# GpSimd's subtractions for the low parts of weights and rows, made in pieces of 256 columns

## The chip, the core and the metric

The kernel runs on one core of a Trainium2 chip. Five engines work side by side from queues of their own: TensorE (PE, matrix products), VectorE (DVE), ScalarE (ACT), GpSimd (POOL) and SyncE (SP), which here only issues transfers. An engine takes its instructions in program order and waits at one until the others that it needs have signalled. The metric is the device time of one execution in microseconds (us), and three runs of a kernel are summed up by their median.

## What is computed

Two layers of a diffusion backbone act on 512 latent tokens of width 1024, with 256 context tokens. The first layer mixes tokens by windowed attention with sink logits, the second by chunked spatial gating, and a SwiGLU block follows each. Every half layer is scaled and shifted by vectors that come from the conditioning vector.

```python
for i in range(DEPTH):                      # DEPTH = 2
    mod_l = silu_c @ ada_w[i] + ada_b[i]    # shift, scale, gate: 6 x 1024
    h_l = modulate(rmsnorm(x, norm_g[i, 0]), sh_ml, sc_ml)
    if kind == 0:
        y_l, y_c = window_sink_mixer(h_l, h_c, a_w_qkv[j], a_w_o[j], ...)
    elif kind == 1:
        y_l, y_c = chunk_gmlp_mixer(h_l, h_c, b_w_in[j], ..., b_w_o[j], ctx_out)
    x = x + g_ml * rmsnorm(y_l, norm_g[i, 1])
    f_l = swiglu(modulate(rmsnorm(x, norm_g[i, 2]), sh_fl, sc_fl), ffn_w_in[i], ffn_w_out[i])
    x = x + g_fl * rmsnorm(f_l, norm_g[i, 3])
```

All of it is float32.

## The kernel before, in words

**A product in three.** TensorE takes a faster float32 form (F32R) that keeps fewer bits, so an operand is split into a high part, which is the operand rounded to that form, and a low part, which is the operand less its high part. A product is then high x high + low x high + high x low, three matmuls (`mm3`, L267 to L270). `high` (L215) is a copy on ACT. `low` (L218) is a subtraction, L219 in the profile, on DVE unless the caller names another engine.

**Who names GpSimd.** Three callers do, and they stand in two stages of the first layer.

- Stage 1 multiplies the latent rows and the context rows by the key and value weights (`kv`, L572), one eighth of the width after the other, while the conditioning vectors of the next eighths are made. Its weights come in units of 128 x 2048, each in two halves of 128 x 1024. After the high part of a half (`ws.high`), `ws.low` makes the low part on GpSimd in one instruction of 1024 columns (L693); there are five such. One `kv` uses 512 columns of such a half.
- Attention works on four blocks of 128 queries and four groups of heads. In between, the query weights and part of the output weights are made ready: GpSimd subtracts halves of 512 columns (L1033 and L1061), fourteen in all.
- `Ada.stack` (L397) splits the summed rows of a conditioning vector, 64 partitions of 1024 columns, three times (`acc_st`; two in attention, one after it).

**The order.** In these two stages the order of the work is written out by hand: `at(time, step, ...)` puts a step into a plan under a name, a table ORDER ranks the names, and `run_plan` emits the steps by rank (a step that the table lacks comes behind, by its time). That is the order on every engine's queue; the times have no other effect.

**What the prediction speaks of.** `norm_in` (L476) scales half the width of a block of 128 context rows, `xin`, on DVE, and `turn_in` (L499) transposes it on TensorE. `modulate0` and `modulated_low` make the high and low parts `HA` of the modulated latent rows; `ada0_done` (L540 and L541) makes their scale and shift from small columns. `Ada.add` (L370) adds up weighted rows of the conditioning weights, loaded as `ada_raw` by SyncE through `dma` (L213). `k_add` (L795) finishes the rotated keys `kr`, which `k_turn` (L808) transposes to `kT`. In attention `rotate` (L726) multiplies queries by the rotary table on GpSimd, `q_split` (L747) subtracts on DVE, `normalise` (L927) multiplies probabilities `p` by the inverse sum on GpSimd, and `turn` (L933) transposes them on TensorE.

Of the kernel before, what the change touches and what calls it, by code (L numbers as in the profile page):

```python
# [7 lines left out]
F32 = mybir.dt.float32  # L8
# [3 lines left out]
ALU = mybir.AluOpType  # L12
# [190 lines left out]
def backbone_kernel(ctx: ExitStack, tc: tile.TileContext, a, out):  # L203
    nc = tc.nc
# [11 lines left out]
        nc.scalar.copy(out=hi, in_=src)  # L216

    def low(lo, hi, src, eng=None):  # L218
        (eng or nc.vector).tensor_tensor(out=lo, in0=src, in1=hi.bitcast(F32), op=ALU.subtract)  # L219

    def split(hi, lo, src):
        high(hi, src)
        low(lo, hi, src)
# [56 lines left out]
    class Stream:  # L280
# [37 lines left out]
        def low(self, u, h, eng, c0=0, c1=D):  # L318
            hi, lo = self.halves[u, h]
            low(lo[:, c0:c1], hi[:, c0:c1], self.raws[u][:, h * D + c0:h * D + c1], eng)  # L320
# [32 lines left out]
    class Ada:  # L353
# [32 lines left out]
        def halve(self, c, eng, of=stage):  # L386
            self.stages[c] = st = of("acc_st")
            high(st[:, 0:512], self.acc[:, c:c + 512])
            low(st[:, 512:], st[:, 0:512], self.acc[:, c:c + 512], eng)
# [280 lines left out]
    for k in range(KC):  # L670
        b, n = start[k], start[k + 1]
        for t in range(NT):
            at(b + .64 * t, kv, k, t)
        for z in ([k - 1] if k else []) + ([k] if k == KC - 1 else []):
            c = b if z < k else b + 1.3
# [303 lines left out]
    c = LEAD  # L979
# [113 lines left out]
    x = hb.tile([P, NT, D], F32, name="x")  # L1093
# [800 lines left out]
    for t in range(NT):  # L1894
        c = VChain(t)
# [149 lines left out]
```

## Time and profile before

| what | value |
|---|---|
| three runs | 1111.84, 1112.92, 1114.41 us; median 1112.92 |
| the profiled execution | 1113.02 us, of which its span is 1111.3 |
| granted clock of TensorE, mean | 0.995 |
| busy: PE, DVE, ACT, POOL | 1088.7, 951.4, 613.0, 246.4 us |
| instructions of POOL | 239 |
| GpSimd's subtractions, L219 | 5 of 128x1024, 14 of 128x512, 3 of 64x1024; 39.3 us together |

The first page gives each engine's busy time. A view by stretch gives the same for a part of the span. A view of groups puts instructions of one line, engine and shape together: their busy time, the mean of one in ns, then the engine's idle time just before them and what ended it. A row of the timeline is a start in us, a duration in us, the engine, the line, the operation, its output and inputs, and in square brackets the idle time before it and what released it; a row of "x2" is two instructions back to back. The chain of waits follows the work that ended last back to what released it. Matmuls overlap, so a matmul of 0.39 us may follow another by 0.23.

### The profile page before, as it was taken

How to read it: one execution, taken by the hardware profiler on the slowest of the kernel's cores; microseconds unless marked ns; L12 is line 12 of the kernel's file. 1: busy time of each engine (PE TensorE's matmuls, PEld its weight loads, DVE VectorE, ACT ScalarE, POOL GpSimd, SP SyncE). 2: the span in 40 equal slices, each digit the busy share in tenths (PEclk: the TensorE clock that was granted, in tenths of full speed). 3: DMA queues.
4: the chain of work that ended last, by engine and by line, in shares of the span. 5: the costliest groups of instructions: out<-in, count | busy, mean ns of one | idle time of the engine just before them, and what ended most of it. 6: DMA issues, size and time to landing. Idle time of an engine off the chain costs nothing.

```text
span 1111.3 us, 17832 instructions
## 1 busy us (share of the span) xinstructions
PE 1088.7 (98%) x6972; PEld 956.4 (86%) x6972; DVE 951.4 (86%) x1417; ACT 613.0 (55%) x1059; POOL 246.4 (22%) x239
## 2 busy tenths in 40 slices
PE   7999999999999999999999999999999999999997
PEld 4688887768899999998888788888899999998876
DVE  5788989868999999997987877988988898879985
ACT  6346777756555555555665634327555545546652
POOL 1316485533700000000320501006500000002400
PEclk9999999999999999999999999999999999999999
DMA  9543432153145556459973286652133343369911
GB/s 367 225 165 106 159 108 81 69 174 114 63 166 190 183 179 208 142 171 314 240 138 114 76 313 214 219 200 96 64 126 135 133 149 120 130 216 321 171 33 75
DMA packets 49016, 179.68 MB, mean 162 GB/s; under 512 B 4890, under 2 KB 9242, under 8 KB 37796
## 3 DMA queue, kind: packets, MB, share of 16 engines
q1 hardware_dynamic: 41300, 163.60, 42.3%
q0 software_dynamic: 7632, 14.95, 7.9%
q8 instruction: 54, 0.88, 0.3%
q14 instruction: 30, 0.25, 0.1%
HBM read 171.71 MB, written 2.10 MB: 156 GB/s over the span
## 4 chain that ended last, share of the span: by engine, by line
PE 84%; DVE 7%; DMA 3%; issue 2%; ACT 2%; POOL 1%; SPq 0%; DVEq 0%; POOLq 0%; ACTq 0%
PE f L1444 33%; PE y L1622 12%; PE y L276 5%; PE v L276 4%; PE y L1649 3%; PE s_ps L900 3%; PE o_ps L953 3%; PE pT_ps L933 3%; DVE w_lo L219 1%; PE u L1856 1%; PE u L1858 1%; PE u L1857 1%; PE q_ps L268 1%; DMA acc<-acc 1%; PE q_ps L270 1%
## 5 line engine op out<-in xcount | busy, mean ns | idle before, releaser
L1444 PE MATMUL f<-H,w_hi 128*128 128x256 f32 x960 | 178.4, 284 | 0.2 <-DVE fc L1455 0.2
L1444 PEld LDWEIGHTS f<-H,w_hi 128*128 128x128 f32 x960 | 149.9, 192 | 1.1 <-DVE fc L1455 0.7
L1444 PE MATMUL f<-H,w_lo 128*128 128x256 f32 x480 | 135.8, 283 | 0.0
L1622 PE MATMUL y<-w_hi,s 128*128 128x512 f32 x448 | 120.1, 389 | 0.0
L1444 PE MATMUL f<-S,w_hi 128*128 128x256 f32 x640 | 118.6, 283 | 0.0
L216 ACT CAST w_hi<-T 128x1024 fp32r<-128x1024 f32 x80 | 83.7, 1047 | 54.1 <-PE f L1444 35.0
L216 ACT CAST w_hi<-w_raw 128x1024 fp32r<-128x1024 f32 x90 | 94.4, 1052 | 30.0 <-PE y L1622 8.9
L1451 ACT COPY fc<-f 128x256 f32<-128x256 f32 x120 | 44.8, 373 | 103.0 <-PE f L1444 100.1
L219 DVE TENSOR_TENSOR w_lo<-w_raw,w_hi 128x1024 fp32r<-128x1024 f32 (+1 forms) x81 | 95.3, 1182 | 6.0 <-ACT w_hi L216 6.0
L1444 PEld LDWEIGHTS f<-S,w_hi 128*128 128x128 f32 x640 | 100.0, 192 | 0.1
L1622 PEld LDWEIGHTS y<-w_hi,s 128*128 128x128 f32 x448 | 84.1, 188 | 17.5
L219 DVE TENSOR_TENSOR w_lo<-T,w_hi 128x1024 fp32r<-128x1024 f32 x80 | 97.4, 1217 | 0.0
L1444 PEld LDWEIGHTS f<-H,w_lo 128*128 128x128 f32 x480 | 92.1, 192 | 0.0
L392 POOL DMA_DIRECT2D acc<-acc x9 | 7.8, 861 | 377.4 <-DVE acc L378 371.7
L1444 PE MATMUL f<-S,w_lo 128*128 128x256 f32 x320 | 90.6, 283 | 0.5 <-DVE w_lo L219 0.5
L378 DVE SCALAR_TENSOR_TENSOR acc<-ada_k,sc,acc 128x1024 f32<-128x1024 f32 x56 | 71.6, 1279 | 10.4 <-DMA ada_k<-in_ada 8.4
L1610 POOL DMA_DIRECT2D t<-in_w x48 | 42.2, 929 | 125.9 <-DMA t<-in_w 58.3
L1622 PE MATMUL y<-w_lo,s 128*128 128x512 f32 x224 | 69.1, 390 | 0.6 <-DVE w_lo L219 0.6
L1444 PE MATMUL f<-H,x 128*128 128x256 f32 x480 | 64.2, 283 | 0.0
L927 POOL TENSOR_SCALAR p<-p,st 128x512 f32<-128x512 f32 (+1 forms) x64 | 53.1, 845 | 47.0 <-DVE st L923 16.2
L276 PE MATMUL y<-w_hi,st 128*128 128x512 f32 x224 | 62.3, 391 | 0.0
L1444 PEld LDWEIGHTS f<-S,w_lo 128*128 128x128 f32 x320 | 61.4, 192 | 0.7 <-DVE w_lo L219 0.7
(255 smaller groups left out, 2855.0 us busy)
## 6 DMA issues: line engine op xcount, KB each, us to landing
w_raw<-in_w SPq DMA_DIRECT2D x67, 1024.0 KB, 5.2
ada_k<-in_ada SPq DMA_DIRECT2D x56, 512.0 KB, 4.9
ada_raw<-in_ada SPq DMA_DIRECT2D x12, 1024.0 KB, 4.9
w<-in_w SPq DMA_DIRECT2D x12, 1024.0 KB, 9.5
t<-in_w POOLq DMA_DIRECT2D x48, 256.0 KB, 6.0
ada<-in_ada SPq DMA_DIRECT2D x8, 1024.0 KB, 6.5
t<-in_w SPq DMA_DIRECT2D x8, 1024.0 KB, 9.1
w_raw<-in_w SPq DMA_DIRECT2D x10, 512.0 KB, 4.8
```

The lines of the kernel that those rows point to most:

```text
L216: nc.scalar.copy(out=hi, in_=src)
L219: (eng or nc.vector).tensor_tensor(out=lo, in0=src, in1=hi.bitcast(F32), op=ALU.subtract)
L276: nc.tensor.matmul(dst, l, w[:, n * 512:(n + 1) * 512], start=first and i == 0, stop=last and i == 2)
L378: nc.vector.scalar_tensor_tensor(out=self.acc, in0=self.raws.pop(k), scalar=sc[:, k:k + 1], in1=self.acc, op0=ALU.mult, op1=ALU.add)
L900: nc.tensor.matmul(dst, self.qT[:, j, :], keys, start=i == 0, stop=i == 1)
L927: nc.gpsimd.tensor_scalar(out=p, in0=p, scalar1=self.st[:, 12 + j:13 + j], scalar2=1.0, op0=ALU.mult, op1=ALU.mult)
L933: nc.tensor.transpose(ps[:, j * P:(j + 1) * P], self.probs[j][:, i * P:(i + 1) * P], ident)
L953: nc.tensor.matmul(self.o[z * HD:(z + 1) * HD, c], v, pt[:, c], start=i < 2, stop=i >= self.nb - 2, tile_position=(0, z * HD), skip_group_ ...
L1444: nc.tensor.matmul(dst, l[:, w], r[:, k, :], start=first and k == 0 and j == 0, stop=k == 3 and j == 2, skip_group_check=True)
L1451: nc.scalar.copy(out=self.c[n][:, i * 256:(i + 1) * 256], in_=self.ps[n, 1 if i == 1 else 0])
L1610: nc.gpsimd.dma_start(out=self.tt[:, p * D + 512 * i:p * D + 512 * (i + 1)], in_=a["w"][F2[self.layer] + 1 + 2 * p + i][:, c:c + 512], acc ...
L1622: nc.tensor.matmul(self.bank7(i, j), st[:, c:c + P], w[:, z * 512:(z + 1) * 512], start=i == 1 and p == 0 and l == 0 and z == 0, stop=p == ...
```

## The change

The subtraction `low` is made in pieces of 256 columns when the engine is GpSimd and the tile has two dimensions. Everything else is as before; lines behind the place move by four.

```diff
     def low(lo, hi, src, eng=None):
-        (eng or nc.vector).tensor_tensor(out=lo, in0=src, in1=hi.bitcast(F32), op=ALU.subtract)
+        n = lo.shape[-1]
+        step = 256 if eng is nc.gpsimd and len(lo.shape) == 2 else n
+        for c in range(0, n, step):
+            v = (lambda x: x[:, c:c + step]) if step < n else (lambda x: x)
+            (eng or nc.vector).tensor_tensor(out=v(lo), in0=v(src), in1=v(hi).bitcast(F32), op=ALU.subtract)
```

The order of instructions on TensorE, VectorE, ScalarE and SyncE stays as it was; 22 instructions of GpSimd become 60. In stage 1, GpSimd's queue before the change runs through the five subtractions of weights up to the first rotary products:

```order
L219 TENSOR_TENSOR w_lo<-w_raw,w_hi 128x1024 [waits DMAHW5_49,Activation_49]
L219 TENSOR_TENSOR w_lo<-w_raw,w_hi 128x1024 [waits DMAHW0_49,Activation_49]
L219 TENSOR_TENSOR w_lo<-w_raw,w_hi 128x1024 [waits Activation_49]
L219 TENSOR_TENSOR w_lo<-w_raw,w_hi 128x1024 [waits DVE_49,DMAHW6_49,PE_49,Activation_49]
L219 TENSOR_TENSOR w_lo<-w_raw,w_hi 128x1024 [waits Activation_49]
L726 TENSOR_TENSOR qr<-qsb,rope 128x8x32 [waits DMAHW4_49,DVE_49,Activation_49]
```

The same stretch of GpSimd's queue with the change:

```order
L223 TENSOR_TENSOR w_lo<-w_raw,w_hi 128x256 [waits DMAHW5_49,Activation_49]
L223 TENSOR_TENSOR w_lo<-w_raw,w_hi 128x256 x3
L223 TENSOR_TENSOR w_lo<-w_raw,w_hi 128x256 [waits DMAHW0_49,Activation_49]
L223 TENSOR_TENSOR w_lo<-w_raw,w_hi 128x256 x3
L223 TENSOR_TENSOR w_lo<-w_raw,w_hi 128x256 [waits Activation_49]
L223 TENSOR_TENSOR w_lo<-w_raw,w_hi 128x256 x3
L223 TENSOR_TENSOR w_lo<-w_raw,w_hi 128x256 [waits DVE_49,DMAHW6_49,PE_49,Activation_49]
L223 TENSOR_TENSOR w_lo<-w_raw,w_hi 128x256 x3
L223 TENSOR_TENSOR w_lo<-w_raw,w_hi 128x256 [waits Activation_49]
L223 TENSOR_TENSOR w_lo<-w_raw,w_hi 128x256 x3
L730 TENSOR_TENSOR qr<-qsb,rope 128x8x32 [waits DMAHW4_49,DVE_49,Activation_49]
```

Each subtraction has become a train of four, of which only the first waits; nothing else has come between them.

On SyncE, the loads behind the subtractions in stage 1, first before and then with the change (a name ahead of _49 is an engine or a transfer queue that the load waits for):

```order
L213 DMA w_raw<-in_w 128x2048 [waits DVE_49,Pool_49]
L213 DMA ada_428<-in_ada 128x2048 [waits DMAHW7_49,PE_49]
L213 DMA ada_raw<-in_ada 128x2048 [waits DMAHW0_49,Pool_49]
L213 DMA ada_raw<-in_ada 128x2048 [waits DMAHW1_49,DMAHW0_49,DVE_49]
L213 DMA ada_raw<-in_ada 128x2048 [waits DMAHW6_49,DMAHW2_49,Pool_49]
```

```order
L213 DMA w_raw<-in_w 128x2048 [waits DVE_49,Activation_49,Pool_49]
L213 DMA ada_434<-in_ada 128x2048 [waits DMAHW7_49,PE_49]
L213 DMA ada_raw<-in_ada 128x2048 [waits DMAHW0_49,Activation_49,Pool_49]
L213 DMA ada_raw<-in_ada 128x2048 [waits DMAHW1_49,DMAHW0_49,DVE_49]
L213 DMA ada_raw<-in_ada 128x2048 [waits DMAHW2_49,DMAHW6_49,Activation_49,Pool_49]
```

The loads stand where they stood; the three that wait for GpSimd now name ACT as well, and wait for the last piece of a train.

In attention, GpSimd's queue from the first split of summed rows to the second pair of weight halves, before the change:

```order
L219 TENSOR_TENSOR acc_st<-acc,acc_st 64x1024 [waits DMAHW1_49,DMAHW6_49,Activation_49,Pool_49]
L927 TENSOR_SCALAR p<-p,st 128x640 [waits DMAHW3_49,DVE_49,Pool_49]
L927 TENSOR_SCALAR p<-p,st 128x640 [waits DMAHW5_49]
L927 TENSOR_SCALAR p<-p,st 128x640 x2
L219 TENSOR_TENSOR w_lo<-w_raw,w_hi 128x512 [waits PE_49,Activation_49]
L219 TENSOR_TENSOR w_lo<-w_raw,w_hi 128x512
```

and with it:

```order
L223 TENSOR_TENSOR acc_st<-acc,acc_st 64x256 [waits DMAHW1_49,DMAHW6_49,Activation_49,Pool_49]
L223 TENSOR_TENSOR acc_st<-acc,acc_st 64x256 x3
L931 TENSOR_SCALAR p<-p,st 128x640 [waits DMAHW3_49,DVE_49,Pool_49]
L931 TENSOR_SCALAR p<-p,st 128x640 [waits DMAHW5_49]
L931 TENSOR_SCALAR p<-p,st 128x640 x2
L223 TENSOR_TENSOR w_lo<-w_raw,w_hi 128x256 [waits PE_49,Activation_49]
L223 TENSOR_TENSOR w_lo<-w_raw,w_hi 128x256 x3
```

The split has become four pieces ahead of the same four normalisations, and the pair of halves four pieces behind them.

## The prediction

> **What bounds the kernel now.** I read the first page, then the busy time by stretch, then the groups of GpSimd (POOL), then the timeline and the chain of waits at each place where a GpSimd subtraction of L219 stands.
>
> ```profile
> span 1111.3 us, 17832 instructions
> PE 1088.7 (98%) x6972; PEld 956.4 (86%) x6972; DVE 951.4 (86%) x1417; ACT 613.0 (55%) x1059; POOL 246.4 (22%) x239
> PE 84%; DVE 7%; DMA 3%; issue 2%; ACT 2%; POOL 1%; SPq 0%; DVEq 0%; POOLq 0%; ACTq 0%
> 0.00:28.00 28.00, 21.65 (x133) 12.68 (x137) 16.05 (x47) 17.45 (x30) 4.81 (x11) 0.94 0.93 366
> 28.00:90.00 62.00, 58.30 (x376) 47.49 (x369) 50.84 (x83) 27.36 (x48) 16.98 (x11) 0.97 0.58 206
> 90.00:244.00 154.00, 152.62 (x1043) 120.44 (x1042) 134.39 (x289) 110.84 (x244) 88.76 (x95) 1.00 0.32 103
> ```
>
> TensorE (PE) is busy 98% of the span and holds 84% of the chain, GpSimd 1%. So a time on GpSimd counts only where PE stands idle or slow for it. The columns of the stretches are length, then busy PE, weight loads, VectorE (DVE), ACT, POOL, the granted clock, and two for DMA. The subtractions lie in 28:90 (stage 1) and 90:244 (attention), and one at 246 us. PE idles 62.00 - 58.30 = 3.70 us in the first and 154.00 - 152.62 = 1.38 us in the second: that is all there is to gain, besides clock.
>
> The first stretch holds one clear stall:
>
> ```profile
> 10.27 0.48 DVE L476 TENSOR_SCALAR xin<-xin,r 128x512 f32<-128x512 f32 x1
> 28.36 2.39 POOL L219 TENSOR_TENSOR w_lo<-w_raw,w_hi 128x1024 fp32r<-128x1024 f32 x1 [11.32 <-ACT w_hi L216]
> 28.48 2.57 DVE L476 TENSOR_SCALAR xin<-xin,r 128x512 f32<-128x512 f32 x1
> 31.19 0.63 PE L499 MATMUL xT<-ident,xin 128*128 128x128 f32 x4 [2.58 <-DVE xin L476]
> ```
>
> DVE's normalisation of a 128x512 half takes 0.48 us alone (10.27) and 2.57 us here. GpSimd started 0.12 us ahead of it, and it ends at 31.05, 0.30 us after GpSimd's instruction (28.36 + 2.39 = 30.75): DVE was held for the whole of the GpSimd instruction. PE needs that half for the transpose at 31.19 and idles 2.58 us. The Trainium skill, SBUF — State Buffer, section Who interferes with whom, says that the two engines share a port pair, which the first to issue keeps for its whole instruction; the pair of rows agrees.
>
> The stall has a tail. The stretches on the grid of the clock:
>
> ```profile
> 8.62:12.04 3.42, 0.66 (x4) 0.42 (x4) 1.39 (x5) 2.29 (x5) 1.34 (x2) 1.00 1.00 400
> 12.04:15.45 3.41, 3.11 (x8) 1.54 (x9) 1.85 (x8) 2.98 (x7) 1.12 (x3) 0.50 1.05 443
> 25.69:29.10 3.41, 2.92 (x25) 1.68 (x23) 3.30 (x11) 2.43 (x5) 0.74 (x1) 1.00 0.98 402
> 29.10:32.52 3.42, 1.33 (x8) 1.24 (x9) 2.61 (x3) 0.72 (x2) 1.66 (x1) 1.00 0.85 299
> 32.52:35.93 3.41, 3.41 (x10) 2.67 (x10) 2.82 (x8) 2.30 (x3) 1.60 (x1) 0.50 1.00 422
> ...
> 33.24 0.43 PE kv L270
> 38.05 0.23 PE kv L270
> ```
>
> After a stretch in which PE was busy for 0.66 us, and after one with 1.33 us, the next 3.41 us were granted half the clock; after 2.92 us it stayed full. In 32.52:35.93 a kv matmul advances the chain by 0.43 us where it later takes 0.23.
>
> **The change part by part.** *The pieces.* 22 instructions become 60: five of 1024 columns and three of 64x1024 become four each, fourteen of 512 become two each.
>
> ```profile
> L219 POOL TENSOR_TENSOR w_lo<-w_raw,w_hi 128x512 fp32r<-128x512 f32 x14 | 19.5, 1396 | 5.6 <-ACT w_hi L216 5.5
> L219 POOL TENSOR_TENSOR w_lo<-w_raw,w_hi 128x1024 fp32r<-128x1024 f32 x5 | 12.3, 2466 | 28.5 <-ACT w_hi L216 20.6 <-PE cols L532 7.9
> L219 POOL TENSOR_TENSOR acc_st<-acc,acc_st 64x1024 fp32r<-64x1024 f32 x3 | 7.5, 2501 | 10.5 <-ACT acc_st L216 10.3
> 77.60 1.43 POOL L726 TENSOR_TENSOR qr<-qsb,rope 128x256 f32<-128x256 f32 x2 [19.73 <-ACT qsb L731]
> 113.42 1.29 POOL L219 TENSOR_TENSOR w_lo<-w_raw,w_hi 128x512 fp32r<-128x512 f32 x1
> ```
>
> The trace has no 256-column subtraction. The nearest rows are qr, a GpSimd instruction of two inputs on 256 elements, two in 1.43 us, and the line through the undisturbed 1024 (2.39) and 512 (1.29) columns: 1.29 - (2.39 - 1.29)/2 = 0.74. I take 0.70 for each of a train, 0.73 for one alone. Four then take 2.80 us for 2.40 (+0.40), two 1.41 for 1.29 (about +0.12): in all 8 x 0.40 + 14 x 0.12 = 4.9 us more on GpSimd. GpSimd is idle for 1111.3 - 246.4 = 864.9 us of the span, which hides it; were GpSimd the bound, the whole 4.9 would show.
>
> *The first subtraction.* The xin that comes 0.12 us after GpSimd now waits for one piece: it ends at 28.36 + 0.73 + 0.30 = 29.39 instead of 31.05, so the transposes start **1.66** us sooner. Its bounds: 0 (DVE is not let in between pieces) and 2.09 (2.57 - 0.48, DVE not held at all). That DVE is let in at the boundary between two GpSimd instructions, the trace shows once in stage 1:
>
> ```profile
> 34.33 5.10 POOL L219 TENSOR_TENSOR w_lo<-w_raw,w_hi 128x1024 fp32r<-128x1024 f32 x2 [3.57 <-ACT w_hi L216]
> 35.62 1.50 DVE L540 TENSOR_SCALAR sb<-cs,cols 128x2 f32<-128x2 f32 x1
> 37.03 2.43 DVE L541 TENSOR_SCALAR sb<-cs,sc,cols 128x2 f32<-128x2 f32 x1
> ```
>
> L540, issued 1.29 us into the first of two subtractions, ended at 37.12, when the second was only starting (34.33 + 5.10/2 = 36.88): it went in between; the next, L541, was held to the end of the second, 39.46.
>
> *The clock.* PE now idles from 28.61 (31.19 - 2.58) to about 29.53, so the stretch 29.10:32.52 would have 3.42 - 0.43 = 2.99 us busy, above the 2.92 after which the clock stayed full. Six kv matmuls of the chain in the half-clock stretch then take 0.23 for 0.43: **1.20** us; bounds 0 and 3.41 / 2 = 1.70. I take the matmuls, since the rest of that stretch runs beside VectorE work that does not depend on the clock. The Trainium skill, TensorE: Matmul & The Clock Gate, section What's actually happening in Part 1, puts the fall to half clock after an idle window of some 3.4 us; the idle time here is 2.58 us and the clock fell all the same, so the rows decide. If the rule held to the letter, the fall would have another cause and stay, which is the first rival's time.
>
> Together PE leads by 1.66 + 1.20 = 2.86 us from 36 us on. *What it gives back.* The rows that decide 54 to 77 us:
>
> ```profile
> 54.34 1.05 ACT L216 CAST w_hi<-w_raw 128x1024 fp32r<-128x1024 f32 x1 [2.54 <-PE kv L270]
> 55.47 2.40 POOL L219 TENSOR_TENSOR w_lo<-w_raw,w_hi 128x1024 fp32r<-128x1024 f32 x1 [5.74 <-ACT w_hi L216]
> 56.14 2.27 DVE L219 TENSOR_TENSOR HA<-hf,HA 128x512 fp32r<-128x512 f32 x1 [0.59 <-ACT HA L554]
> 57.89 0.33 SPq L213 DMA_DIRECT2D ada_raw<-in_ada  x1
> 63.02 1.29 DVE L370 SCALAR_TENSOR_TENSOR acc<-ada_raw,sc,acc 128x1024 f32<-128x1024 f32 x1 [0.30 <-DMA ada_raw<-in_ada]
> 73.83 2.35 DVE L795 TENSOR_TENSOR kr<-ksrc 128x1024 f32<-128x1024 f32 x2
> 76.57 1.03 PE L808 MATMUL kT<-ident,kr 128*128 128x128 f32 x8
> ```
>
> The fifth subtraction ends at 57.87 and its end releases SyncE's ada_raw load at 57.89, with one more ada_raw load, the rope table and a load of weights queued behind it on SP. DVE waits for that load at 63.02, then runs nearly back to back to kr, which ends at 76.18; PE takes kr at 76.57, so 0.39 us of slack. With the change the subtraction is asked for 2.86 us sooner, takes 0.40 more, and lets HA (2.27 us here) in between two pieces, which I put at 0.60 more of the 0.68 that HA takes alone:
>
> ```profile
> 54.29 0.68 DVE L219 TENSOR_TENSOR HA<-hf,HA 128x512 fp32r<-128x512 f32 x1
> ```
>
> The load starts 1.00 us later against the lead; the slack covers 0.39: give-back **0.61**, so the lead is 2.25 at 77 us. Its bounds: 0 (DVE done early elsewhere) and 1.0. On SP the three loads behind a GpSimd subtraction now wait for ACT as well; that is the cast which the subtraction itself has waited for, so it costs nothing. The other two such loads start 0.40 us later each, and no PE wait in the stage follows from them.
>
> *Attention.* Here a pair of w_lo halves on GpSimd meets the scaling of q (L747) on DVE, and the last two rows are, with the 0.53 us of the row above them, all that PE is seen to wait for in the stage:
>
> ```profile
> 107.83 2.97 POOL L219 TENSOR_TENSOR w_lo<-w_raw,w_hi 128x512 fp32r<-128x512 f32 x2
> 107.90 1.76 DVE L747 SCALAR_TENSOR_TENSOR qs<-qr,qs 128x512 fp32r<-128x512 f32 x1
> 113.64 0.50 PE L405 MATMUL ada_ps<-acc_st,ones 128*128 128x512 f32 x1 [0.53 <-ACT qT L755]
> ...
> PE q_ps L268 <- ACT qsb L731: 0.3, 1, 0.3
> PE s_ps L900 <- ACT p L911: 0.3, 1, 0.3
> ```
>
> L747 waits for half of the pair, and through DVE and ACT behind it PE idles 0.53 us at 113.64. With a first piece of 0.71 instead of 1.29 it ends 0.58 sooner; I take two thirds of the 0.53, **0.35** gained. Bounds for the stage: 1.38 gained (all PE idle time), and a loss priced in the second rival. All three waits name ACT, none GpSimd. The subtraction at 246 us lies in a stretch without PE idle time (18.00 of 18.00 busy in 244:262): nothing.
>
> ```profile
> 244.00:262.00 18.00, 18.00 (x80) 14.43 (x78) 10.76 (x13) 10.81 (x16) 2.40 (x1) 1.00 0.52 171
> ```
>
> **Sum:** -1.66 - 1.20 + 0.61 - 0.35 = -2.60 us. The profiled execution took 1113.02 us, 1.72 around its span of 1111.3, and stands 0.10 above the median of the runs, 1112.92. So 1113.02 - 2.60 = **1110.4**; taken from the median it would be 1110.3. What a measurement of this kernel can tell from no change is about 0.2%, 2.2 us, so faster begins at 1110.7, and slower at 1115.1.
>
> **The rivals.** *The half-clock stretch stays.* The lead of 1.66 stands, the clock falls as before, because the clock's grid lies differently in another execution or because a busy time just under 3 us is not enough. Against it: 2.92 us of busy time was enough, and 2.99 is forecast. For it: only two falls are on record, so the limit lies anywhere between 1.33 and 2.92, and the grid's place is known for one execution. Time: 1113.02 - 1.66 + 0.61 - 0.35 = 1111.6.
>
> *Slower: GpSimd's queue in attention.* A piece that meets a running DVE instruction waits for it. Every new boundary hands the ports to a DVE instruction that stands ready, and DVE is busy 134.39 of 154 us there. GpSimd also makes the normalised probabilities (p, L927), which PE transposes. In its order a subtraction stands directly ahead of a p in ten places; each p comes later by 0.12 of pieces and by one DVE instruction let in, 0.68 as HA:
>
> ```profile
> L927 POOL TENSOR_SCALAR p<-p,st 128x512 f32<-128x512 f32 (+1 forms) x64 | 53.1, 845 | 47.0 <-DVE st L923 16.2
> ```
>
> If PE had to wait for it at six of the ten, that is 6 x 0.80 = 4.8 us, and 1113.02 - 2.25 + 4.8 = 1115.6. Against it: PE waits at no p in the trace, and GpSimd sits idle 47 us ahead of its p's, waiting for others. For it: the slack of a p to its transpose is not in any one row, and 1.38 us of PE idle in 154 says that the order is tight. It decides from the third such wait on, where the lead is used up. The Trainium skill, SBUF — State Buffer, section Who interferes with whom, says that issue order decides who blocks, so that a GpSimd instruction can as well be the one that waits; the w_lo pair at 107.83, 2.97 us where two alone take 2.58, agrees.
>
> *No gain.* DVE is not let in between pieces of one train: 1113.02 + 0.40 at the fifth subtraction less the slack of 0.39 = 1113.0. Against it stands L540.
>
> *More than forecast.* No give-back at the load and all of attention's idle time gone: 1113.02 - 2.86 - 1.38 = 1108.8.
>
> **How the numbers follow.** Forecast 0.48 (its own range 1109.3 to 1111.5: 0.35 of it faster by over 0.2%, 0.13 within); clock stays 0.18, within; slower 0.19 (0.15 slower, 0.04 within, for fewer waits); no gain 0.05, within; more than forecast 0.10, faster. Faster 0.45, same 0.40, slower 0.15. The range 1108.6 to 1115.0 holds the forecast, the clock, no gain, nearly all of the larger gain and a third of the slower case, some 0.85.
>
> **What would show it.** In the changed profile: xin at about 28.5 lasting 0.8 to 1.0 us instead of 2.57; the transposes at about 29.5; no clock of 0.50 after 29 us (the dip at 12 us stays); 60 subtractions of about 0.70 us; the ada_raw load of 57.89 near 56.0 with kT near 74.3; ada_ps of 113.64 with next to no wait ahead. Wrong would be a xin still over 2 us, a half-clock stretch at 32, or PE waits at pT_ps (L933 before the shift of lines) for p.

## The result, and the profile after

Ten runs of the changed kernel have a median of 1110.45 us (1108.93 to 1112.68), ten of the kernel before 1113.44 us (1111.82 to 1115.55). The ratio is 0.9973 with a 95% interval of 0.9963 to 0.9983: 3.0 us faster, between 1.9 and 4.1. The forecast was 1110.4 us. The profiled execution took 1109.84 us, 3.18 below that of before, and its span is 1108.1 us. No ratio below counts the profiled execution of e1, which took 1333.0 us at a granted clock of 0.752.

The first page of the changed kernel, its two stretches (length, then busy PE, weight loads, DVE, ACT, POOL, the granted clock and two columns for DMA), and its groups of GpSimd subtractions:

```profile
PE 1088.0 (98%) x6972; PEld 955.4 (86%) x6972; DVE 946.2 (85%) x1417; ACT 614.0 (55%) x1059; POOL 257.4 (23%) x277
28.00:90.00 62.00, 59.63 (x396) 48.99 (x389) 49.54 (x91) 29.52 (x54) 21.07 (x26) 1.00 0.61 221
90.00:244.00 154.00, 153.07 (x1037) 120.13 (x1037) 132.02 (x285) 110.85 (x240) 94.09 (x117) 1.00 0.33 105
L223 POOL TENSOR_TENSOR w_lo<-w_raw,w_hi 128x256 fp32r<-128x256 f32 x48 | 38.7, 831 | 27.8 <-ACT w_hi L216 23.1 <-PE cols L536 4.7
L223 POOL TENSOR_TENSOR acc_st<-acc,acc_st 64x256 fp32r<-64x256 f32 x12 | 9.2, 799 | 10.5 <-ACT acc_st L216 10.3
```

PE is busier in both stretches (59.63 for 58.30, 153.07 for 152.62 us), and the clock of the first is 1.00 for 0.97. GpSimd has become 11.0 us busier. Its subtractions take 38.7 + 9.2 = 47.9 us for 39.3: a piece takes 0.80 to 0.83 us on average and not 0.70. Most pieces take 0.72 to 0.78 us, but those beside which a VectorE instruction is let in count that as their own time: the piece at 52.93, beside HA at 52.91, takes 1.27.

The first stall, in the timeline of the changed kernel and in its stretches on the grid of the earlier figures:

```profile
28.33 3.04 POOL L223 TENSOR_TENSOR w_lo<-w_raw,w_hi 128x256 fp32r<-128x256 f32 x4 [11.50 <-ACT w_hi L216]
28.44 0.95 DVE L480 TENSOR_SCALAR xin<-xin,r 128x512 f32<-128x512 f32 x1
29.54 0.63 PE L503 MATMUL xT<-ident,xin 128*128 128x128 f32 x4 [0.96 <-DVE xin L480]
29.10:32.52 3.42, 2.98 (x16) 2.55 (x17) 2.61 (x6) 1.65 (x3) 2.28 (x4) 1.00 0.76 286
32.52:35.93 3.41, 3.41 (x27) 2.16 (x26) 3.34 (x8) 2.54 (x4) 2.93 (x4) 1.00 0.99 417
33.08 1.07 PE L525 MATMUL rows<-ada,s 128*32 128x256 f32 x16
```

What these rows show: xin at 0.95 us for 2.57, its end at 28.44 + 0.95 = 29.39, the transposes at 29.54 for 31.19, and no half clock behind them: PE was busy for 2.98 us of the stretch in which it had been busy for 1.33. The sixteen row products that follow start at 33.08, against this row of before:

```profile
36.32 1.07 PE L521 MATMUL rows<-ada,s 128*32 128x256 f32 x16
```

That is 3.24 us sooner, 1.65 from the stall and 1.59 from the clock. I call this difference, between the starts of the same PE instruction before and after, the lead of PE. At the load of ada_raw and at kr the changed kernel shows:

```profile
52.23 3.54 POOL L223 TENSOR_TENSOR w_lo<-w_raw,w_hi 128x256 fp32r<-128x256 f32 x4 [4.77 <-ACT w_hi L216]
55.80 0.33 SPq L213 DMA_DIRECT2D ada_raw<-in_ada  x1
60.72 1.28 DVE L374 SCALAR_TENSOR_TENSOR acc<-ada_raw,sc,acc 128x1024 f32<-128x1024 f32 x1 [1.51 <-DMA ada_raw<-in_ada]
71.53 2.36 DVE L799 TENSOR_TENSOR kr<-ksrc 128x1024 f32<-128x1024 f32 x2
73.31 1.04 PE L812 MATMUL kT<-ident,kr 128*128 128x128 f32 x8
```

The train of four took 3.54 us, the load was issued 2.09 us sooner than before and VectorE's sum behind it started 2.30 sooner, so VectorE fell about 0.95 us behind the lead of PE. But PE took kr at 73.31, 3.26 us sooner than before and ahead of the end of the row of kr (71.53 + 2.36 = 73.89). The row is two instructions of 1024 columns, and the eight transposes of 128 columns need only the first of them, which ends near 72.7.

In attention, first the rows of the changed kernel at the places where the lead of PE changes, then three rows of before that belong to them:

```profile
104.65 1.22 DVE L751 SCALAR_TENSOR_TENSOR qs<-qr,qs 128x512 fp32r<-128x512 f32 x1
105.30 4.22 POOL L223 TENSOR_TENSOR w_lo<-w_raw,w_hi 128x256 fp32r<-128x256 f32 x4
109.85 0.50 PE L409 MATMUL ada_ps<-acc_st,ones 128*128 128x512 f32 x1
138.66 1.50 DVE L374 SCALAR_TENSOR_TENSOR acc<-ada_raw,sc,acc 128x1024 f32<-128x1024 f32 x1 [1.01 <-DMA ada_raw<-in_ada]
141.71 0.63 PE L937 MATMUL pT_ps<-ident,p 128*128 128x128 f32 x4 [0.35 <-DVE pt L944]
181.56 0.21 DVE L921 TENSOR_TENSOR st<-st,sinks 128x4 f32<-128x4 f32 x1
181.73 1.42 POOL L223 TENSOR_TENSOR w_lo<-w_raw,w_hi 128x256 fp32r<-128x256 f32 x2
188.16 0.50 PE L904 MATMUL s_ps<-khi,qT 128*128 128x512 f32 x1
```

```profile
144.89 0.60 PE L933 MATMUL pT_ps<-ident,p 128*128 128x128 f32 x4
184.64 1.30 DVE L917 TENSOR_TENSOR st<-st,sinks 128x4 f32<-128x4 f32 x1
191.74 0.50 PE L900 MATMUL s_ps<-khi,qT 128*128 128x512 f32 x1
```

The lead grows to 113.64 - 109.85 = 3.79 us at ada_ps, whose idle time of 0.53 is gone. It shrinks to 144.89 - 141.71 = 3.18: there VectorE waits 1.01 us for a load of ada_raw, and PE waits for VectorE's copy behind it. With a second wait of 0.16 us, at 145.28, it is 148.35 - 145.28 = 3.07. The load was issued 3.70 us sooner than before (131.96 for 135.66), but VectorE got it only 6.7 us after its issue, where before VectorE used it 5.55 us after its issue without waiting. The lead grows again to 191.74 - 188.16 = 3.58, because a small VectorE instruction (st) takes 0.21 instead of 1.30 us: it now starts 0.17 us ahead of GpSimd's pair at 181.73, where before the two started within 0.02 us of one another (184.64 and 184.66) and st was held. The span ends 3.2 us sooner, so some 0.4 us is given back after 248 us.

That load is late in other executions too, and neither the pieces nor the size of the lead goes with it. In e3, where attention's subtractions are whole and the lead is 2.1 us, and in e12, where they are in pieces and the lead is 3.7 us:

```profile
139.92 1.83 DVE L370 SCALAR_TENSOR_TENSOR acc<-ada_raw,sc,acc 128x1024 f32<-128x1024 f32 x1 [0.68 <-DMA ada_raw<-in_ada]
143.30 0.63 PE L936 MATMUL pT_ps<-ident,p 128*128 128x128 f32 x4 [0.35 <-DVE pt L943]
```

```profile
137.49 1.86 DVE L378 SCALAR_TENSOR_TENSOR acc<-ada_raw,sc,acc 128x1024 f32<-128x1024 f32 x1
```

PE has this wait in three profiles (the change, e3 and e6), where VectorE got the load 6.4 to 6.7 us after its issue. In e10 and e11 VectorE waited for it, until 6.1 and 6.3 us after its issue, and PE did not wait. In before, e4, e7, e9 and e12 VectorE used it by 5.6 us after its issue, and neither engine waited. Why the load sometimes takes longer is open.

### The profile page after: what moved, and what is told of

Read it like the earlier page. It is cut to its first block, busy times and chain, and to the rows that moved or that the text cites. A ratio compares the mean times of both kernels' runs of the same rounds, so it can differ in the third digit from the quotient of the medians.

```text
span 1108.1 us, 17873 instructions
## 1 busy us (share of the span) xinstructions
PE 1088.0 (98%) x6972; PEld 955.4 (86%) x6972; DVE 946.2 (85%) x1417; ACT 614.0 (55%) x1059; POOL 257.4 (23%) x277
## 4 chain that ended last, share of the span: by engine, by line
PE 66%; DVE 4%; POOL 1%; issue 1%; ACT 1%; DMA 0%; POOLq 0%; DVEq 0%; SPq 0%; ACTq 0%
PE f L1448 35%; PE y L1626 13%; PE y L1653 4%; PE v L280 4%; PE y L280 2%; PE u L1862 1%; PE u L1860 1%; PE u L1861 1%; POOL tmp L1165 1%; DVE w_lo L223 1%; PE hT L1176 1%; PE fa L272 1%; PE fa L274 1%; PE fa L273 1%; PE mix L1875 1%
```

## The experiments

Each ratio is to the kernel before on the same chip, with its 95% interval. A ratio of 0.001 is 1.1 us.

| run | what is cut or moved | median us | ratio | interval |
|---|---|---|---|---|
| e1 | the first subtraction in four | 1110.92 | 0.9981 | 0.9971 to 0.9990 |
| e2 | all others in 256, and six of VectorE | 1114.51 | 1.0010 | 0.9998 to 1.0022 |
| e3 | none; matmuls on zeros in PE's gap | 1112.35 | 0.9990 | 0.9982 to 0.9999 |
| e4 | none; xin ahead of HA | 1109.80 | 0.9968 | 0.9956 to 0.9980 |
| e5 | attention and behind, and six of VectorE | 1115.07 | 1.0014 | 1.0003 to 1.0025 |
| e6 | e4, and the first subtraction in four | 1110.46 | 0.9977 | 0.9965 to 0.9988 |
| e7 | the first subtraction in two | 1112.22 | 0.9986 | 0.9978 to 0.9995 |
| e8 | all in pieces of 128, and six of VectorE in eight | 1117.05 | 1.0040 | 1.0028 to 1.0052 |
| e9 | attention and behind alone | 1111.82 | 0.9986 | 0.9978 to 0.9995 |
| e10 | all in pieces of 128 | 1111.86 | 0.9988 | 0.9979 to 0.9997 |
| e11 | the change and e4 | 1110.00 | 0.9967 | 0.9956 to 0.9978 |
| e12 | e4 and e9 | 1108.69 | 0.9958 | 0.9946 to 0.9970 |

**The first subtraction alone (e1).** In every kernel with cuts, `low` takes a list of widths, and `ws.low` gives one by unit, half and column:

```diff
         def low(self, u, h, eng, c0=0, c1=D):
             hi, lo = self.halves[u, h]
-            low(lo[:, c0:c1], hi[:, c0:c1], self.raws[u][:, h * D + c0:h * D + c1], eng)
+            cut = (256,) * 4 if (u, h) == (KV0, 1) else None
+            low(lo[:, c0:c1], hi[:, c0:c1], self.raws[u][:, h * D + c0:h * D + c1], eng, cut)
```

> Only the first of GpSimd's subtractions (1024 columns, stage 1) is made in four pieces, the other 21 are whole. If the change's gain is that one stall with its half-clock stretch: xin takes about 0.95 us, the transposes start near 29.5 us, no clock of 0.50 after 29 us, PE leads by about 3.2 us at 37 us; the idle time of 0.5 us ahead of ada_ps stays; time 2.4 to 3.2 us below the kernel before. If shorter holds all over the two stages bring the gain: less than 1.5 us below.

It is 2.1 us faster (1.1 to 3.2), in the median a little less than the 2.4 to 3.2 expected. There is no profile of it to read, so only the time answers: this one subtraction is worth more than half of the gain by the medians, but the interval is too wide to say what is left for the others.

**All but the first (e2).**

```diff
+            cut = (256,) * ((c1 - c0) // 256) if eng is nc.gpsimd and (u, h) != (KV0, 1) else None
...
-            low(st[64:128, :], st[64:128, :], self.acc[64:128, :], eng)
+            low(st[64:128, :], st[64:128, :], self.acc[64:128, :], eng, (256,) * 4)
```

> All of GpSimd's subtractions in pieces of 256 except the first one, which is whole. If the gain is the first stall with its half-clock stretch: xin 2.57 us, transposes at 31.2 us, and the time within 1 us of the kernel before (the 0.5 us at ada_ps gained, as much lost later). If the other pieces bring it: 1.5 to 3 us below.

The time is 1.1 us above before (0.2 below to 2.5 above), but it decides nothing, because its last line also cuts the subtractions of 64x1024 that VectorE makes behind attention: six in the trace, though the expectation of e9 says five. By e5 against e9, below, that cut costs about 3 us, so without it e2 would be an estimated 2 us below before, with more than 1 us of doubt to each side: the other pieces may well bring a part of the gain. It told something else, though. Its stretches around the stall, on the grid on which its own clock changes:

```profile
29.23:32.64 3.41, 1.53 (x9) 1.39 (x10) 2.60 (x3) 0.49 (x1) 1.45 (x1) 1.00 0.84 296
32.64:36.05 3.41, 3.41 (x29) 2.11 (x28) 3.37 (x8) 2.50 (x4) 1.79 (x3) 1.00 1.00 422
```

xin was held for 2.57 us and PE idled 2.60 us, and no half clock followed. Four profiles have this stall whole: before, e2, e5 and e9. In e5, and then in e9, on their own grids:

```profile
26.94:30.35 3.41, 1.31 (x18) 0.42 (x16) 3.41 (x4) 2.05 (x4) 2.36 (x1) 1.00 1.02 383
30.35:33.76 3.41, 2.94 (x9) 2.58 (x10) 2.14 (x5) 0.77 (x2) 0.04 (x1) 0.50 0.95 373
```

```profile
26.57:29.98 3.41, 2.08 (x21) 0.98 (x19) 3.38 (x8) 2.85 (x5) 1.56 (x1) 1.00 1.02 412
29.98:33.39 3.41, 2.14 (x12) 1.87 (x13) 2.60 (x4) 0.43 (x2) 0.84 (x1) 1.00 0.79 305
```

The grid lies differently in each execution. Where most of the gap falls into one stretch, so that PE is busy for only 1.33 us (before) or 1.31 (e5), half clock follows; with 1.53 (e2), or a gap shared by two stretches (e9), it does not. So the clock's part of the gain is there in some executions and not in others. Four profiles are too few to say how often, but every execution has its mean granted clock on record. One stretch of 3.41 us at half clock lowers the mean over 1111 us by 0.0015. The mean is 0.9965 over 122 executions of the kernels that have the whole stall (before, e2, e5, e9), and 0.9976 over 93 of those that do not have it whole or have PE busy in it (the change and all other runs). The difference of 0.0011 is some 0.7 of such a stretch for each execution, so the 1.59 us is worth about 1.1 on the median, an estimate.

**Work for PE in the gap (e3).**

```diff
     def turn_in(t, h):
...
+        if t == 4 and h == 1:
+            fill(ps)
+            fill(ps)
```

> The kernel before with two matmuls on zeros, 128x512, whose result is overwritten, put ahead of the transposes that wait for the held xin. xin stays held for 2.57 us and the transposes start at 31.2 us. If the half-clock stretch follows from the low busy time and costs by itself: clock 1.00 from 32.5 to 36 us, PE leads by 1.2 to 1.7 us at 37 us, time 1.0 to 1.7 us below. If the stretch costs nothing because VectorE's work sets the pace there: within 0.4 us.

Rows of e3, the zeros' matmuls and the transposes on PE, the held xin, and the stretch behind:

```profile
28.03 2.58 DVE L476 TENSOR_SCALAR xin<-xin,r 128x512 f32<-128x512 f32 x1
28.11 1.98 PE L484 MATMUL xT<-idle 128*128 128x512 f32 x4
30.67 0.66 PE L502 MATMUL xT<-ident,xin 128*128 128x128 f32 x4 [0.58 <-DVE xin L476]
32.52:35.93 3.41, 3.41 (x28) 2.13 (x27) 3.38 (x6) 2.57 (x4) 2.08 (x1) 1.00 1.02 429
```

The stall is whole, the clock stays, and the kernel is 1.1 us faster (0.1 to 2.0). The half clock costs by itself, and its price on the median agrees with the 1.1 above. The first part of this execution was 0.5 us sooner than before's, so the start of its transposes says nothing on its own.

**Another order instead of pieces (e4).** In the table of the order:

```diff
-modulated_ctx_1 whigh_0_1 modulated_low_1
-ada0_fetch_6 ada0_rows_3 norm_in_4_1 turn_in_4_1
+modulated_ctx_1 whigh_0_1 norm_in_4_1 modulated_low_1
+ada0_fetch_6 ada0_rows_3 turn_in_4_1
```

> The kernel before with one change of order on VectorE: xin is made ahead of HA's low part instead of behind it; all subtractions whole. xin starts near 27.9 us, before GpSimd has begun, and takes 0.48 us; the transposes start near 28.6. If GpSimd's instruction holds whatever VectorE work comes during it: HA's low part is held in xin's place until about 31.05, the first kv matmul waits for it until about 31.2, and the gain is at most 0.7 us. If it was xin alone: the kv matmuls start near 29.3, and the gain is 2 us or more.

```profile
28.14 0.48 DVE L476 TENSOR_SCALAR xin<-xin,r 128x512 f32<-128x512 f32 x1
28.54 0.69 DVE L219 TENSOR_TENSOR HA<-hf,HA 128x512 fp32r<-128x512 f32 x1
28.63 2.85 POOL L219 TENSOR_TENSOR w_lo<-w_raw,w_hi 128x1024 fp32r<-128x1024 f32 x1 [11.32 <-ACT w_hi L216]
30.11 1.52 DVE L562 TENSOR_SCALAR hfc<-cnT,sb 128x256 f32<-128x256 f32 x1
32.28 0.50 PE L268 MATMUL kv<-w_hi,HA 128*128 128x512 f32 x1 [0.53 <-DVE xnT L506]
```

The gain is 3.6 us (2.2 to 4.9), as large as the change's, with no piece at all. The reason that I had given for a small gain did not come to pass, by 0.09 us: HA began before GpSimd, so GpSimd was the one held (2.85 us for 2.39), and the whole instruction then held hfc (1.52 us for 0.41), which cost PE 0.53 us at 32.28 and no more. The hold had not gone; it had moved to an instruction with slack.

**Attention alone, first with VectorE's cut (e5), then without (e9).**

```diff
+            cut = (256,) * ((c1 - c0) // 256) if eng is nc.gpsimd and u >= Q0 + 2 else None
...
-            low(st[64:128, :], st[64:128, :], self.acc[64:128, :], eng)
+            low(st[64:128, :], st[64:128, :], self.acc[64:128, :], eng, (256,) * 4 if eng is nc.gpsimd else None)
```

This is e9; e5 has `(256,) * 4` alone at the end.

> Pieces of 256 only in attention and behind it (the fourteen halves and the three splits of summed rows); the five subtractions of stage 1 are whole. If attention is worth as little as the change's trace has it (0.5 us gained at ada_ps, 0.6 lost at a transpose near 145): within 0.8 us of the kernel before. If the shorter holds of VectorE in attention bring a part of the gain: 1 us or more below. If GpSimd's longer queue costs: 1 us or more above. xin is held for 2.57 us again; whether half clock follows depends on where the clock's grid lies in the profiled execution.

> As e5_attention_only, but only GpSimd's subtractions are cut: e5 (and e2, e8 with it) also cut five subtractions of 64x1024 that VectorE makes behind attention, and lost about 2.5 us near 757 us. If that cut was the loss: about 2.5 us below e5 against the same kernel before, so 0 to 1.5 us below before, with 0.5 us gained at ada_ps and 0.4 near 190 us. If pieces on GpSimd in attention cost: again 1 us or more above before.

e5 is 1.6 us slower than before (0.3 to 2.8), e9 1.6 us faster (0.6 to 2.4), and the only difference is VectorE's six subtractions. One of them in before, and the same in e5:

```profile
712.27 1.22 DVE L219 TENSOR_TENSOR acc_st<-acc,acc_st 64x1024 fp32r<-64x1024 f32 x1
```

```profile
711.70 1.44 DVE L225 TENSOR_TENSOR acc_st<-acc,acc_st 64x256 fp32r<-64x256 f32 x4
```

The pieces themselves take 0.22 us more, 1.3 for the six. The rest goes with a wait of PE near 757 us, of which e5 has this row:

```profile
PE y L283 <- DVE m L1883: 1.4, 1, 1.4
```

Three of three profiles with VectorE's cut have this wait at 1.4 to 1.6 us, and one of ten without it has it at over 1 us (e11, 1.3). That the cut brings it more often is likely by that count; how it does was not tried, and the cost of the cut in time, about 3 us, rests on e5 against e9.

e9's waits of PE from 90 to 262 us, all of them:

```profile
PE q_ps L275 <- ACT qsb L739: 0.3, 1, 0.3
PE s_ps L908 <- ACT p L919: 0.3, 1, 0.3
```

The wait at ada_ps is gone, and the wait at the transpose near 145 us, which the change has, is not there: it goes with the late load, not with the pieces. So attention's pieces are worth about what their two places are, 0.53 us at ada_ps and 0.50 at st (from 3.08 to 3.58 us of lead in the change, from 2.04 to 2.54 in e9), and the time of e9 (1.6 us) agrees with that within its interval. By time alone e9's 1.6 us and e1's 2.1 do not say which part is the larger. By the traces it is the first stall, with 1.65 us and about 1.1 for its clock.

**The first subtraction in two (e7).** The cut is `(512,) * 2` where e1 has `(256,) * 4`.

> The first subtraction in two pieces of 512 instead of four of 256; all others whole. If a held instruction waits for just the piece that it meets: xin takes 1.29 + 0.30 - 0.12 = 1.47 us, the transposes start near 30.1, PE idles 1.5 us and no half clock follows; 1.1 us from the stall and what the clock is worth on the median, in all 1.5 to 2.7 us below the kernel before. If any boundary frees VectorE at once: xin near 0.95, as with four pieces.

```profile
28.41 1.49 DVE L484 TENSOR_SCALAR xin<-xin,r 128x512 f32<-128x512 f32 x1
```

That is the forecast to 0.02 us: a held instruction waits for the piece that it meets, plus 0.30. The time is 1.6 us below before (0.6 to 2.4).

**Pieces of 128, with VectorE's cut (e8) and without (e10).**

```diff
+            cut = (128,) * ((c1 - c0) // 128) if eng is nc.gpsimd else None
...
-            low(st[64:128, :], st[64:128, :], self.acc[64:128, :], eng)
+            low(st[64:128, :], st[64:128, :], self.acc[64:128, :], eng, (128,) * 8 if eng is nc.gpsimd else None)
```

This is e10; e8 has `(128,) * 8` alone at the end.

> All of GpSimd's subtractions in pieces of 128 columns, twice as many boundaries as the change. If pieces cost only time in which GpSimd is idle: xin 0.7 us, PE 0.2 us sooner, time within 0.7 us of the change, 1109.8 to 1111.2. If each boundary costs on the path (a VectorE instruction let in, later normalised probabilities): 1.5 us or more above the change, and PE waits at the transposes of p.

> As e8_pieces_of_128, but only GpSimd's subtractions are cut. If e8 lost 2.5 us to VectorE's cut and the rest to PE's waits for p: 1 to 3 us above before, PE waits 2 to 3 us for p at the transposes, so pieces of 128 cost 4 us or more against pieces of 256. If all of e8's loss was VectorE's cut: within 1 us of the change.

The waits of PE in e10 from 90 to 262 us, the longest first, and its stretches:

```profile
PE pT_ps L941 <- POOL p L935: 2.5, 2, 1.5
...
28.00:90.00 62.00, 59.89 (x398) 48.81 (x391) 48.22 (x90) 29.50 (x54) 25.03 (x46) 1.00 0.61 221
90.00:244.00 154.00, 150.76 (x1027) 118.16 (x1027) 133.28 (x284) 109.76 (x239) 100.11 (x151) 1.00 0.32 101
```

Here is the cost that the second rival had named: PE waits twice for probabilities that GpSimd normalises too late, 2.5 us together, and is busy for 150.76 of 154 us where the change has 153.07. GpSimd is busy for 100.11 us there, for 94.09 in the change and 88.76 before. This execution took 1114.69 us, 2.8 above e10's median, so it may show more than the usual cost; the profile of e8 has the same two waits, 2.6 us together. The stall of stage 1 is cured as well as in the change, and more than half of the gain is lost again: e10 is 1.3 us faster than before (0.3 to 2.3), the change 3.0. Neither expectation held: I had looked for 1 to 3 us above before and had left the first stall's gain out of it, and against the change e10 is 1.7 us slower by the two ratios, taken on two chips. e8 against e10 says that VectorE's six subtractions in eight pieces cost 5.8 us, also across two chips.

**Both remedies, and the best kernel (e6, e11, e12).** e6 has e4's order and e1's cut; e11 e4's order and the change (GpSimd's subtractions alone); e12 e4's order and e9's cuts.

> Both remedies of the first stall: xin ahead of HA's low part on VectorE, and the first subtraction in four pieces; all others whole. The transposes start near 28.8 us as with the swap alone. If the context rows' scaling (hfc, 1.52 us with the swap alone, 0.41 undisturbed) is then let in between pieces, the wait of 0.5 us of the kv matmul at 32.3 goes: 0.4 to 0.6 us below the swap alone, about 1109.3. If the swap leaves nothing for the pieces: the same as the swap alone within 0.3 us.

> The change, and xin ahead of HA's low part on VectorE. If the swap's sooner transposes (28.8 for 29.5 us) carry through: 0.3 to 0.8 us below the change, about 1109.9. If the later load of ada_raw near 145 us takes it back: the same as the change within 0.3 us.

> xin ahead of HA's low part, and pieces of 256 in attention and behind it alone; the five subtractions of stage 1 are whole. If the swap replaces the first subtraction's pieces and the other four in stage 1 give nothing: the same as e11 within 0.5 us. If the stage 1 pieces still matter: 0.5 us or more above e11.

e6 came out 2.6 us below before (1.3 to 3.9), not below e4's 3.6: the wait of 0.53 us at 32.28 was gone from its trace, and the time did not follow. The intervals of the two overlap, so which is faster stays open. e11 is 3.7 us below before (2.4 to 4.9), where 1109.9 us was expected and 1110.00 measured; e12 is 4.7 below (3.3 to 6.0). That is 1.0 us below e11 where the same within 0.5 was expected, but the intervals overlap. e12 has the lowest ratio of all: the order in stage 1, pieces of 256 in attention, and whole subtractions in stage 1. Its first stall is gone without a piece:

```profile
28.01 0.48 DVE L484 TENSOR_SCALAR xin<-xin,r 128x512 f32<-128x512 f32 x1
90.00:244.00 154.00, 153.57 (x1040) 120.75 (x1039) 132.43 (x284) 110.77 (x240) 94.76 (x118) 1.00 0.33 107
```

Against the change's 0.9973 (0.9963 to 0.9983) its 0.9958 (0.9946 to 0.9970) lies lower, with intervals that just overlap, on another chip. That e12 beats the change is likely, not shown.

## Why the prediction was right

The total was right, 3.0 us for a forecast of 2.6, and so was its main step, that xin is held for one piece instead of the whole instruction. The other terms were right in part, and that they came out near the total is partly luck: a give-back of 0.61 us that did not come makes room for 0.4 lost at the end.

- *The first subtraction, 1.66 us:* 1.65. xin ended at 29.39 as worked out, the transposes came at 29.54. e7 shows the rule behind it on another size (1.49 us for 1.47 expected).
- *The clock, 1.20 us:* in the two profiled executions 1.59, since I had counted six kv matmuls and left out the two column transposes and the partly slowed ones. But the first rival holds in part, for the kernel before: two of four profiles with the stall show no half clock, and by the mean clocks about 0.7 of all executions have it, so the median holds some 1.1. The step was mis-sized in both ways, and the two nearly cancel.
- *The give-back, 0.61 us:* none. The delay was right (VectorE starts 0.95 us later against the lead, for 1.00 forecast), the slack was not: I had taken the end of a row of two kr instructions as what PE waits for, and PE needs the first. The first of the two ended near 75.0 us before (73.83 + 2.35 / 2), so the slack was about 1.5 us and not 0.39.
- *Attention, 0.35 us:* 0.32 in the profile (the lead goes from 3.26 to 3.58), but as 0.53 + 0.51 gained and 0.72 lost. I had seen the first (and taken two thirds) and missed the held st at 184.64. The loss is the late load of ada_raw, for which PE waits in e3 and e6 with attention's subtractions whole, and does not wait in e11 and e12 with pieces and a larger lead, so that this sum agrees is luck.
- *Nothing behind 248 us:* 0.4 us was given back there. Other kernels give back more in that part: the lead over before falls from 3.2 us at 262 us to 2.0 at the end in e4, from 2.8 to 1.6 in e7, from 4.3 to 2.8 in e12 and from 5.2 to 2.3 in e11. Why is not shown.
- *GpSimd's own time, 4.9 us:* 8.6 in the subtractions (47.9 for 39.3), because the VectorE work that gets in between pieces counts as theirs, and 11.0 in all. No wait of PE at a p follows at 256 columns, as forecast.

Of the rivals, the slower one is a true mechanism that begins to cost between pieces of 256 and of 128. The Trainium skill, SBUF — State Buffer, section Who interferes with whom, says that issue order decides who blocks; e4 agrees, where GpSimd, 0.09 us behind HA, was the one that waited (2.85 us for 2.39). The Trainium skill, GPSIMD Engine Reference, section 3.1 (Elementwise — side-by-side cycle accounting), gives GpSimd some 2.6 cycles for an element of two inputs; at 1.2 GHz, which the page uses, that would be an estimate of 1.11 us for 512 columns, and the rows of before agree with the step from 512 to 1024 (2.39 - 1.29 = 1.10).

## What to carry to other kernels

Where GpSimd and VectorE hold one another, look for the one VectorE instruction that the critical engine waits for while a long GpSimd instruction runs: cutting that GpSimd instruction shortens the hold to one piece, and putting the VectorE instruction ahead of it, where it fits, removes it without a piece. Cut to the size where the hold hurts no more and stop there, since every boundary also lets VectorE ahead of GpSimd's own queue. Read a row of several instructions by the one that the waiter needs. And do not take a lead at one place for the gain: part of it may be given back behind.

## What the runs showed that was not expected

- The half clock behind a gap of 2.6 us is a matter of how the grid of 3.41 us lies in the execution: it followed busy times of 1.33 and 1.31 us, and not 1.53 or 2.08. The busy time of the profile does not draw the line exactly: an earlier fall in the changed kernel, on its own grid, followed 1.57. So a kernel with this stall can differ by 1.6 us from one execution to the next for this reason alone. The row of that earlier fall, and the one behind it:

```profile
9.77:13.18 3.41, 1.57 (x9) 1.11 (x10) 2.44 (x8) 2.37 (x5) 1.38 (x3) 1.00 1.03 423
13.18:16.59 3.41, 3.35 (x13) 2.27 (x12) 1.72 (x5) 2.61 (x7) 2.44 (x4) 0.50 1.02 430
```

- Six VectorE subtractions cut into four pieces each, with nothing else changed, cost about 3 us (e5 against e9, each against before on its own chip), of which the pieces' own time is 1.3.
